# A two-layer encoder trunk on one Trainium2 core: queries placed by DMA, half of the FFN's sums moved into the projection ahead of it, and one pair of weights kept

## The chip, the cores and the metric

The kernel runs on one core of a Trainium2 chip. A core has TensorE for matrix products (PE in the profile, its weight loads PEld), VectorE (DVE), ScalarE (ACT), GpSimd (POOL) and SyncE (SP), which here only issues transfers. Each engine works through its own instructions in order and waits for the others by semaphores. The metric is the time of one execution on the device in microseconds (us); lower is better.

## The reference

One inference step for 1024 prompt tokens and 32 sample tokens of width 1024, two layers. Layer 0 mixes the tokens with a matrix-memory recurrence of 8 heads, layer 1 with windowed attention of 16 query heads over 2 key and value heads of 64. After each mixer comes a SwiGLU FFN (inner width 2816), and after each of the four sub-layers a normalisation:

```python
x = layer_norm(DEEPNORM_ALPHA * x + mix, ln_g[layer, 0], ln_b[layer, 0])
x = layer_norm(DEEPNORM_ALPHA * x + swiglu(x, w_gu[layer], w_down[layer]), ln_g[layer, 1], ln_b[layer, 1])

def swiglu(x, w_gu, w_down):
    g, u = jnp.split(x @ w_gu, 2, axis=-1)
    return (jax.nn.silu(g) * u) @ w_down
```

All is in float32, and the kernel returns the tokens after layer 1, the recurrence's states and the last keys and values.

## The kernel before

**Products.** A float32 operand is kept as two parts, a high one (a cast, on ACT) and a low one (the rest, a subtraction on DVE or POOL), and a product of two such operands is three matmuls, high by high, high by low, low by high (lines L360 to L362, `gemm`). The 1056 tokens lie along the columns, in transposed form: 8 tiles of 128 features (k) by 1056 columns. `ACT` (act) holds the values, `SX` (sx) their two parts.

**The order of the work.** The code is recorded as it is written, and `Weave` mixes it: a task is a generator that yields a pause in planned us of TensorE time, and every step of a `gemm` ticks that clock, so a task's instructions are put between matmuls. `drain` records a task's remaining part at once. Every engine then keeps this order. No wait or length seen on the chip changes it.

**Weights** (class `Weights`, L159 to L202). Units of 512 KB are loaded in a fixed order by SP into three raw buffers. Each unit is split into two halves, whose parts lie in one of five slots, or in a buffer of their own (`W.home`). A pair of units of the FFN makes seven factors for a fast 2 by 2 block product (seven products in place of eight). `done` frees a slot; while `W.ahead` is set, the next half is split some 1.7 planned us after the last one.

**The projection after a mixer** (`mixer_out`, L1135). The tokens go in four quarters of 264 columns; for each, 8 gemms of 24 matmuls, and then the quarter's normalisation as a task (`ln_task`, L421 to L474) that runs beside the next quarter's gemms: the mean by a matmul (L421), centring, squares, the variance by a matmul (L437), the scaling, and the split into sx (L468 on ACT, L474 on DVE and POOL). `squared` holds the quarters whose variance has been recorded. Of the fourth quarter's weights the first six units have their home in `E` (the tile ex).

**The FFN** (`ffn`). Of 22 inner tiles the first two are made plainly (`up_plain`, L1251 and L1253): a visit to tile i and token half c is four gemms of 24 matmuls, with the two units of that tile. The visits go (c 0, i 0), (c 0, i 1), (c 1, i 0), (c 1, i 1), and each visit loads and splits its two units, so each tile's units are loaded twice; these splits' low parts are DVE's (L202). From the third tile on, the block product is used (`up_tile`); its inputs are not only quarters of the tokens but sums of them: with x11, x21 the two feature halves of a half's first quarter and x12, x22 those of its second,

- t3 = x22 - x12, t2 = t3 + x11, t4 = x21 - t2, t1 = x12 - x11.

`sums` makes these for one half c, in steps of two tiles (128 x 528), as a task: a subtraction or addition on DVE into one of two buffers in z (L1287 to L1293), a cast on ACT (L1277), and the low part by turns on DVE and POOL (L1274). t2, t3 and t4 go to ex, t1 into sx in the place of x12, once the half's plain visits are done. Both tasks start after the fourth quarter's variance has been recorded, the second at the third visit, after `drain(tasks[3])`. The first fused tile uses them in the order t2, t4, t1, t3 (`summed`).

**Attention in layer 1.** The queries of a pair of heads j and a column block g (384, 384 and 288 columns) are a group; `q_group` projects it and writes Q so that a head's 64 features of high and of low parts stand in one 128-partition operand: ACT and DVE write 64 partitions each time, four operations (L1580 to L1585). The first four groups (block 0) are made while the last normalisation of layer 0 still runs; 20 more are made while the attention task works on the groups before, three units of 128 queries each (`scores` L1669 and L1675, `soft`, `turn` L1713 to L1717, `values`, `place` L1739). `q_made` tells the attention 2.0 planned us after a group that it may be used.

Of the kernel before, what the change touches and what calls it, by code (L numbers as in the profile page):

```python
# [16 lines left out]
P = 128  # L17
# [17 lines left out]
FIRST, TAIL = 2, 4  # L35
ALPHA = float((2 * DEPTH) ** 0.25)
# [204 lines left out]
def kernel(ctx: ExitStack, tc: tile.TileContext, A, O):  # L241
# [346 lines left out]
    def norm_tail(li, run, box, final=False):  # L588
# [3 lines left out]
        for g, (cols, (c, zs)) in enumerate(QUARTERS):  # L592
# [19 lines left out]
            tasks.append(wv.launch(ln_task(box[0].z, box[0].lnps, QUARTERS[g], li, last, final)))  # L612
        return tasks
# [437 lines left out]
    class Mixer(ExitStack):  # L1051
# [3 lines left out]
        def __init__(self, closing, us):  # L1055
# [8 lines left out]
            for i, u in enumerate(us):  # L1064
                for f in range(2):
                    W.home[u, f] = [self.E[:, h, 2 * i + f, : D // 2] for h in range(2)]

# [50 lines left out]
    def mixer_out(us, li, lx, opening=None, before=None):  # L1118
# [31 lines left out]
    def ffn(layer, li, tasks, lx, final):  # L1150
# [16 lines left out]
        def natural(k0, par):  # L1167
            return lambda c: SX[:, :, k0 : k0 + H, (2 * c + par) * N4 : (2 * c + par + 1) * N4]

        def extra(i):  # L1170
            return lambda c: E[:, :, H * i : H * (i + 1), c * N4 : (c + 1) * N4]

        X = {"x11": natural(0, 0), "x21": natural(H, 0), "x22": natural(H, 1), "t1": natural(0, 1)}
        extras = ("t2", "t3", "t4")
        X.update((o, extra(i)) for i, o in enumerate(extras))
# [62 lines left out]
        def up_plain(i, c):  # L1238
# [3 lines left out]
            for u in (ug, uu):  # L1242
                for par in range(2):
# [4 lines left out]
                    if par:  # L1248
                        W.done(u)
# [4 lines left out]

        plain = [False, False]
        made = []

        def sums(c):


            def x(k, par):
                return ACT[:, k : k + 2, group(2 * c + par)]

            todo = [(o, k) for k in range(0, H, 2) for o in ("t3", "t2", "t4")] + [("t1", k) for k in range(0, H, 2)]
            bufs = [Z[:, i : i + 2, c, :] for i in (7, 9)]
            while (li - 1, 3) not in squared:
                yield 0.3

            def halve(s, low):
                if 0 <= s < len(todo):  # L1270
                    o, k = todo[s]
                    d = X[o](c)[:, :, k : k + 2, :]
                    if low:
                        (nc.vector if s & 1 else nc.gpsimd).tensor_sub(d[:, 1], bufs[s % 2], d[:, 0].bitcast(F32))  # L1274
                        made.append((c, o))
                    else:
                        nc.scalar.copy(d[:, 0], bufs[s % 2])  # L1277

            for s in range(len(todo) + 2):
                halve(s - 2, True)  # L1280
                if s < len(todo):
                    o, k = todo[s]
                    while o == "t1" and not plain[c]:
                        yield 0.3
                    t, before = bufs[s % 2], bufs[(s - 1) % 2]
                    if o == "t3":
                        nc.vector.tensor_sub(t, x(k + H, 1), x(k, 1))  # L1287
                    elif o == "t2":
                        nc.vector.tensor_add(t, before, x(k, 0))
                    elif o == "t4":  # L1290
                        nc.vector.tensor_sub(t, x(k + H, 0), before)
                    else:
                        nc.vector.tensor_sub(t, x(k, 1), x(k, 0))  # L1293
                halve(s - 1, False)
                yield 2.6
# [64 lines left out]
        for c in range(2):  # L1360
            if c:
                wv.drain(tasks[3])
# [583 lines left out]
```

## Time and profile before

| | |
|---|---|
| median of three runs | 2261.14 us (2257.0 to 2265.25) |
| the profiled execution | 2258.92 us |
| its span | 2257.1 us |
| mean granted TensorE clock | 0.994 of full |
| PE busy | 2192.4 us, 97% |
| DVE, ACT, POOL busy | 66%, 45%, 48% |

The span runs from the first to the last instruction of the profiled execution; the time holds a little more around it. In rows of groups the number after x is the count, then come busy us, the mean of one in ns, and the idle time of the engine just before, with what ended it. Rows of waits give the total, the number and the longest. Rows in the order of time begin with start and length in us. Rows of a stretch give for each engine busy us and instructions, then the granted clock, the DMA engines' busy share and GB/s. An `L` with a number is a line of the kernel.

Layer 0's projection and normalisations lie at about 390 to 500 us, its FFN from there to 1175; the queries, keys and values and the attention at 1190 to 1455, layer 1's FFN start at about 1530.

### The profile page before, as it was taken

The numbers are of one execution on the slowest core, as the hardware profiler recorded it, in microseconds if no ns is written. First come the engines' busy times: TensorE is split into PE (matmuls) and PEld (weight loads), VectorE is DVE, ScalarE is ACT, GpSimd is POOL, SyncE is SP. The second block draws the span as 40 slices with busy tenths as digits, with TensorE's granted clock in tenths as the row PEclk, the third lists the DMA queues.
The fourth block names the chain that finished last, engine by engine and source line by source line (L and its number), as shares of the span: only waits on it lengthen the run. The fifth ranks groups of instructions, "written<-read, shape, count | busy, mean of one in ns | idle before, by whom it ended". The sixth has DMA issues, their size and how long they took to land.

```text
span 2257.1 us, 44139 instructions
## 1 busy us (share of the span) xinstructions
PE 2192.4 (97%) x17086; PEld 2152.2 (95%) x17086; DVE 1490.2 (66%) x2850; ACT 1016.2 (45%) x2285; POOL 1076.8 (48%) x999
## 2 busy tenths in 40 slices
PE   9999999999999999999998999899999999999997
PEld 9899999998999999999997998899999999999997
DVE  4465577778566665566667789887666665466657
ACT  4443345464444444322246788656444444422124
POOL 2544331016666666544326775412666666654422
PEclk9999999999999999999999999999999999999999
DMA  4222112211434443696424211421344344397712
GB/s 148 76 51 69 53 39 94 87 48 67 163 135 143 152 149 138 233 329 230 154 77 139 79 60 44 136 74 47 115 153 149 133 148 154 126 343 249 256 50 77
DMA packets 167394, 291.52 MB, mean 129 GB/s; under 512 B 16593, under 2 KB 123145, under 8 KB 167185
## 3 DMA queue, kind: packets, MB, share of 16 engines
q1 hardware_dynamic: 162832, 284.38, 37.1%
q10 hardware_dynamic: 4352, 4.33, 0.5%
q8 instruction: 134, 2.20, 0.4%
q14 instruction: 76, 0.61, 0.1%
HBM read 203.89 MB, written 82.94 MB: 127 GB/s over the span
## 4 chain that ended last, share of the span: by engine, by line
PE 80%; DVE 8%; ACT 4%; DMA 3%; issue 3%; POOL 1%; SPq 0%; ACTq 0%; DVEq 0%; POOLq 0%
PE A L360 9%; PE A L362 9%; PE A L361 9%; PE d L360 9%; PE d L362 9%; PE d L361 9%; PE B L360 7%; PE B L361 7%; PE B L362 7%; PE T L1713 1%; DMA sx<-hs_t 1%; DVE wl L202 1%; DMA wr<-in_dn 1%; DVE ex L1274 1%; PE T L904 1%
## 5 line engine op out<-in xcount | busy, mean ns | idle before, releaser
L202 POOL TENSOR_TENSOR wl_s<-wr,wh_s 128x512 fp32r<-128x512 f32 x224 | 316.6, 1434 | 241.0 <-ACT wh_s L200 169.0
L360 PE MATMUL d<-sx,wh 128*128 128x264 f32 (+2 forms) x1068 | 341.1, 319 | 2.2 <-DVE z L1253 1.5
L362 PE MATMUL d<-sx,wl 128*128 128x264 f32 (+2 forms) x1068 | 326.5, 306 | 7.7 <-DVE wl L202 5.5
L361 PE MATMUL d<-sx,wh 128*128 128x264 f32 (+2 forms) x1068 | 325.7, 305 | 2.0 <-DVE sx L474 1.1
L200 ACT CAST wh_s<-wr 128x512 fp32r<-128x512 f32 x224 | 135.4, 617 | 317.0 <-DVE wr L177 289.1
L360 PE MATMUL A<-sx,wh_s 128*128 128x264 f32 x896 | 255.2, 285 | 2.8 <-ACT z L1338 2.8
L361 PE MATMUL A<-sx,wh_s 128*128 128x264 f32 x896 | 254.8, 284 | 0.0
L362 PE MATMUL A<-sx,wl_s 128*128 128x264 f32 x896 | 254.7, 284 | 0.0
L362 PEld LDWEIGHTS d<-sx,wl 128*128 128x128 f32 x1068 | 201.7, 189 | 10.1 <-DVE wl L202 7.1
L360 PEld LDWEIGHTS d<-sx,wh 128*128 128x128 f32 x1068 | 202.4, 189 | 6.0 <-issue 2.2
L361 PEld LDWEIGHTS d<-sx,wh 128*128 128x128 f32 x1068 | 202.5, 190 | 4.3 <-POOL sx L474 1.5
L202 POOL TENSOR_TENSOR wl_a<-wr,wh_a 128x512 fp32r<-128x512 f32 x112 | 169.1, 1516 | 51.4 <-ACT wh_a L200 49.8
L202 POOL TENSOR_TENSOR wl<-wr,wh 128x512 fp32r<-128x512 f32 (+2 forms) x75 | 100.1, 1343 | 173.9 <-ACT wh L200 151.3
L360 PE MATMUL d<-sx,ex 128*128 128x264 f32 x624 | 180.7, 290 | 0.4 <-ACT sx L390 0.2
L362 PE MATMUL d<-sx,ex 128*128 128x264 f32 x624 | 177.9, 285 | 3.1 <-DVE ex L202 2.6
L361 PE MATMUL d<-sx,ex 128*128 128x264 f32 x624 | 177.3, 284 | 0.2 <-DVE sx L391 0.2
L360 PEld LDWEIGHTS A<-sx,wh_s 128*128 128x128 f32 x896 | 169.0, 189 | 3.3 <-ACT z L1338 3.3
L362 PEld LDWEIGHTS A<-sx,wl_s 128*128 128x128 f32 x896 | 169.4, 189 | 0.0
L361 PEld LDWEIGHTS A<-sx,wh_s 128*128 128x128 f32 x896 | 169.0, 189 | 0.0
L1693 POOL TENSOR_SCALAR s<-s,st 128x256 f32<-128x256 f32 (+1 forms) x144 | 125.5, 884 | 67.4 <-DVE st L1691 54.7
L1208 POOL TENSOR_TENSOR z<-z 128x528 fp32r<-128x528 f32 x76 | 105.2, 1384 | 107.2 <-issue 55.5
L1207 ACT CAST z<-z 128x528 fp32r<-128x528 f32 x136 | 85.9, 631 | 95.9 <-DVE z L1220 46.0
(334 smaller groups left out, 7389.7 us busy)
## 6 DMA issues: line engine op xcount, KB each, us to landing
wr<-in_gu SPq DMA_DIRECT2D x96, 512.0 KB, 4.6
hs_x<-z SPq DMA_DIRECT2D x72, 528.0 KB, 2.8
hs_t<-z SPq DMA_DIRECT2D x64, 528.0 KB, 4.0
sx<-hs_x SPq DMA_DIRECT2D x112, 264.0 KB, 6.0
sx<-hs_t SPq DMA_DIRECT2D x64, 264.0 KB, 5.9
ex<-hs_t SPq DMA_DIRECT2D x64, 264.0 KB, 6.1
wr<-in_dn SPq DMA_DIRECT2D x32, 512.0 KB, 5.5
ex<-hs_x SPq DMA_DIRECT2D x32, 264.0 KB, 6.1
```

What stands on the lines that cost most here:

```text
L200: self.nc.scalar.copy(hi, r)
L202: eng.tensor_sub(lo, r, hi.bitcast(F32))
L360: nc.tensor.matmul(out, ah, bh, start=start and k == 0, stop=False, **kw)
L361: nc.tensor.matmul(out, ah, bl, start=False, stop=False, **kw)
L362: nc.tensor.matmul(out, al, bh, start=False, stop=stop and k == last, **kw)
L904: nc.tensor.matmul(pc[:, : 2 * (DV + 1)], keys, vt[j][:L, c], start=True, stop=True)
L1207: nc.scalar.copy(hi.bitcast(F32R), buf(s))
L1208: eng.tensor_sub(lo.bitcast(F32R), buf(s), hi)
L1274: (nc.vector if s & 1 else nc.gpsimd).tensor_sub(d[:, 1], bufs[s % 2], d[:, 0].bitcast(F32))
L1693: nc.gpsimd.tensor_scalar_mul(p[:R, h, lo:256], p[:R, h, lo:256], st[:R, 2, h : h + 1])
L1713: nc.tensor.transpose(pt[:nk, i, h, :R], p[:R, h, c : c + nk], ident[:R, :R])
```

## The change

Five places change.

- **Visits.** They go (0, 0), (0, 1), (1, 1), (1, 0). The second plain tile's two units are loaded and split once and held over two visits (four of five slots); the first tile's are loaded twice as before.
- **Sums of the first half.** `sums` moves out of `ffn`. For half 0 it is started at the head of the fourth quarter's projection, after the second quarter's normalisation has been recorded to its end, with two buffers of its own (su) in a small pool. The six units in E lie in another order, so that the places of t2 and t4 come free first; `lx.left` counts the units that have been used, and a step waits, when recorded, until its place is free. From the seventh step on it waits for the fourth quarter's variance.
- **Order of the sums.** t3's base is made without a split first (`raw`), for t2 and t4; t3 itself is made again and split after them, then t1. So each half has ten steps on DVE and not eight, and as many casts and low parts as before. The pauses are 2.4 planned us for half 0 and 2.2 for half 1, from 2.6.
- **Half 1** starts, as before, at the third visit after `drain(tasks[3])`, with its buffers in z.
- **Queries.** ACT makes the high part (qh) and DVE the low part (ql) of all 128 partitions in one operation each; a task then issues four transfers from SP, each of 64 partitions, into Q. `q_made` waits 4.0 planned us. Before the attention begins, the last of the first four groups' transfers has been recorded.

```diff
+VISITS = [(0, i) for i in range(FIRST)] + [(1, i) for i in reversed(range(FIRST))]
@@ add_ffn
-        for c in range(2):
-            for i in range(FIRST):
-                up[i, c] = [add("gu", 2 * (layer * FT + i) + k) for k in range(2)]
+        for c, i in VISITS:
+            held = up.get((i, 1 - c)) if i == FIRST - 1 else None
+            up[i, c] = held or [add("gu", 2 * (layer * FT + i) + k) for k in range(2)]
@@ Mixer
-            for i, u in enumerate(us):
+            self.made, self.plain, self.left = [], [False, False], 0
+            for i, u in zip((0, 4, 1, 5, 2, 3), us):
@@ sums (moved out of ffn)
-            todo = [(o, k) for k in range(0, H, 2) for o in ("t3", "t2", "t4")] + [("t1", k) for k in range(0, H, 2)]
-            while (li - 1, 3) not in squared:
-                yield 0.3
+        todo = [(o, k) for k in range(0, H, 2) for o in ("raw", "t2", "t4")]
+        todo += [(o, k) for o in ("t3", "t1") for k in range(0, H, 2)]
+        for s in range(len(todo) + 2):
+            if not c and s >= 6:
+                while (li, 3) not in squared:
+                    yield 0.3
+            halve(s - 2, True)
+            if s < len(todo):
+                o, k = todo[s]
+                while o == "t1" and not lx.plain[c]:
+                    yield 0.3
+                while not c and lx.left < {"t2": 1, "t4": 2}.get(o, 0) + k:
+                    yield 0.3
...
+            halve(s - 1, False)
+            yield pause
@@ mixer_out, run
+            if g == 3:
+                lx = box[0]
+                lx.sums = ExitStack()
+                su = lx.sums.enter_context(pool("sums"))
+                bufs = [new(su, f"su{i}", [P, 2, N4])[:] for i in range(2)]
+                wv.drain(lx.norms[1])
+                lx.comb = wv.launch(sums(lx, li, 0, bufs, 2.4))
...
+                if g == 3 and (u, 0) in W.home:
+                    box[0].left += 1
@@ up_plain
-                    if par:
+                    if par and (c or i < FIRST - 1):
                         W.done(u)
@@ ffn
-            combs.append(wv.launch(sums(c)))
-            for i in range(FIRST):
-                up_plain(i, c)
-            plain[c] = True
+        combs = [lx.comb]
+        for c, i in VISITS:
+            if (c, i) == (1, FIRST - 1):
+                wv.drain(tasks[3])
+                combs.append(wv.launch(sums(lx, li - 1, 1, [Z[:, i : i + 2, 1, :] for i in (7, 9)], 2.2)))
+            up_plain(i, c)
+            lx.plain[c] = (c, i) in (VISITS[FIRST - 1], VISITS[-1])
@@ q_group
-        nc.scalar.activation(q[0:64, 0, :n], ps[0:64], AF.Copy, scale=sc)
-        nc.scalar.activation(q[64:128, 1, :n], ps[64:128], AF.Copy, scale=sc)
...
+        nc.scalar.activation(h, ps, AF.Copy, scale=sc)
+        nc.vector.scalar_tensor_tensor(l, ps, sc, h.bitcast(F32), op0=ALU.mult, op1=ALU.subtract)
+
+        def place():
+            yield 1.0
+            for i in range(2):
+                own, other = slice(64 * i, 64 * i + 64), slice(64 - 64 * i, 128 - 64 * i)
+                nc.sync.dma_start(q[own, i, :n].bitcast(F32), h[own].bitcast(F32))
+                nc.sync.dma_start(q[other, i, :n].bitcast(F32), l[own].bitcast(F32))
+
+        return wv.launch(place())
@@ main
+    wv.drain(placing)
...
     def q_made():
-        yield 2.0
+        yield 4.0
```

Lines from about 290 on have other numbers in the changed kernel: L202 is L203 there, L426 L427, L1135 L1202, L1253 L1315, L1274 L1100, L1277 L1103, L1287 L1118, L1289 L1120, L1291 L1122, L1293 L1124.

DVE in the fourth quarter's projection of layer 0, before (L1135 adds a gemm's result to act; L430, L433 and L600 are a normalisation's):

```order
L1135 SCALAR_TENSOR_TENSOR act<-act,d_5737 128x264
L426 TENSOR_TENSOR act<-ln_5717,act 128x2x264
L430 TENSOR_TENSOR z_4627<-z_4627 128x2x264
L202 TENSOR_TENSOR wl_0_5787<-wr_5062,wh_0_5786 128x512
L430 TENSOR_TENSOR z_4627<-z_4627 128x2x264
L1135 SCALAR_TENSOR_TENSOR act<-act,d_5773 128x264
L600 TENSOR_TENSOR z_4627<-act 128x2x264
L433 TENSOR_TENSOR z_4627<-z_4627 128x264
L1135 SCALAR_TENSOR_TENSOR act<-act,d_5810 128x264
```

The same place in the changed kernel:

```order
L1202 SCALAR_TENSOR_TENSOR act<-act,d_5743 128x264
L427 TENSOR_TENSOR act<-ln_5723,act 128x2x264
L431 TENSOR_TENSOR z_4627<-z_4627 128x2x264
L1120 TENSOR_TENSOR su_675_5673<-su_674_5672,act 128x528
L203 TENSOR_TENSOR wl_0_5794<-wr_5062,wh_0_5793 128x512
L431 TENSOR_TENSOR z_4627<-z_4627 128x2x264
L1202 SCALAR_TENSOR_TENSOR act<-act,d_5779 128x264
L601 TENSOR_TENSOR z_4627<-act 128x2x264
L1122 TENSOR_TENSOR su_674_5672<-act,su_675_5673 128x528
L434 TENSOR_TENSOR z_4627<-z_4627 128x264
L1100 TENSOR_TENSOR ex_4623<-su_675_5673,ex_4623 128x2x264
L1118 TENSOR_TENSOR su_675_5673<-act 128x528
```

Sums of the first half (su) and a low part (L1100 into ex) now stand among the normalisation's work; from the quarter's first gemm to its last they are seven rows.

DVE at the third visit of the plain tiles in layer 0, before:

```order
L474 TENSOR_TENSOR sx<-act,sx 128x2x264
L1274 TENSOR_TENSOR ex_4623<-z_4627,ex_4623 128x2x264
L1287 TENSOR_TENSOR z_4627<-act 128x2x264
L1253 TENSOR_TENSOR z_4627<-z_4627,d_6199 128x264
L202 TENSOR_TENSOR wl_1_6240<-wr_6011,wh_1_6239 128x512
L1287 TENSOR_TENSOR z_4627<-act 128x2x264
L202 TENSOR_TENSOR wl_0_6265<-wr_6082,wh_0_6264 128x512
L1289 TENSOR_TENSOR z_4627<-z_4627,act 128x2x264 x2
L1274 TENSOR_TENSOR ex_4623<-z_4627,ex_4623 128x2x264
L1291 TENSOR_TENSOR z_4627<-act,z_4627 128x2x264 x2
L202 TENSOR_TENSOR wl_1_6314<-wr_6082,wh_1_6313 128x512
```

And in the changed kernel:

```order
L475 TENSOR_TENSOR sx<-act,sx 128x2x264
L1315 TENSOR_TENSOR z_4627<-z_4627,d_6206 128x264
L1124 TENSOR_TENSOR su_674_5672<-act 128x528
L1118 TENSOR_TENSOR z_4627<-act 128x2x264
L1120 TENSOR_TENSOR z_4627<-z_4627,act 128x2x264
L1100 TENSOR_TENSOR ex_4623<-su_675_5673,ex_4623 128x2x264
L1124 TENSOR_TENSOR su_675_5673<-act 128x528
L1122 TENSOR_TENSOR z_4627<-act,z_4627 128x2x264
L203 TENSOR_TENSOR wl_1_6307<-wr_5765,wh_1_6306 128x512
L1100 TENSOR_TENSOR ex_4623<-z_4627,ex_4623 128x2x264
```

Fewer low halves of weights (wl) stand here, and the first half has only t3 and t1 left. From the fourth norm's scaling (L447) to the first fused tile's first addition (L1326) 48 instructions stood on DVE, now 41 do: 3 low halves of weights and not 7, 13 sums and not 15, 6 low parts of sums and not 7, the rest alike.

SP where the first group of the second column block is made, before:

```order
L1774 DMA out_p_v<-act 128x128
L1775 DMA out_s_v<-act 128x32
L159 DMA wr_14805<-in_wqb 128x1024
L1607 DMA bt_14893<-in_bias 128x2x256
L1608 DMA sb_14894<-in_bias 32x2x160
L159 DMA wr_14936<-in_wqb 128x1024
```

And in the changed kernel:

```order
L1799 DMA out_p_v<-act 128x128
L1800 DMA out_s_v<-act 128x32
L160 DMA wr_14811<-in_wqb 128x1024
L1608 DMA Q_14868<-qh_14869 64x384
L1609 DMA Q_14868<-ql_14870 64x384
L1608 DMA Q_14868<-qh_14869 64x384
L1609 DMA Q_14868<-ql_14870 64x384
L160 DMA wr_14919<-in_wqb 128x1024
```

The group's four transfers stand between two weight loads; the bias loads come after the second group's transfers.

More of the change, by code (lines that the diff above doesn't have):

```diff
@@ L1165, in bank @@
             return new(px.pool[tag], tag, [P, 2, 512], bufs=2)[:, :, :N4]
[L1167 to L1173, printed above, removed]
+        X = seven(E)
         extras = ("t2", "t3", "t4")
-        X.update((o, extra(i)) for i, o in enumerate(extras))
         def tiles(t):
@@ L1253, in up_plain @@
                         nc.vector.tensor_mul(t, t, ps)
[L1255 to L1262, printed above, removed]
-            todo = [(o, k) for k in range(0, H, 2) for o in ("t3", "t2", "t4")] + [("t1", k) for k in range(0, H, 2)]
-            bufs = [Z[:, i : i + 2, c, :] for i in (7, 9)]
-            while (li - 1, 3) not in squared:
-                yield 0.3
[L1269 to L1295, printed above, removed]
         tail = []
@@ L1373, in summed @@
             for c in range(2):
-                wv.drain(combs[c], lambda: o != "t1" and made.count((c, o)) == 2)
+                wv.drain(combs[c], lambda: o != "t1" and lx.made.count((c, o)) == 2)
             if o == "t1":
+                lx.sums.close()
                 staging.append(wv.launch(stage(0)))
@@ L1578, in q_group @@
         q = Q[j, g] = new(pb, "Q", [P, 2, 384], F32R, bufs=4)
+        h, l = (new(pb, tag, [P, 384], F32R, bufs=2)[:, :n] for tag in ("qh", "ql"))
         sc = -(HD ** -0.5)
[L1580 to L1587 removed]
+        nc.scalar.activation(h, ps, AF.Copy, scale=sc)
[7 more added lines that the diff above has]
+        return wv.launch(place())
     ck = new(pb, "ck", [P, P])
@@ L1627 @@
     for j in range(4):
-        q_group(j, 0)
+        placing = q_group(j, 0)
         W.done(U_QB[0][j])
```

41 lines of the change are left out of this document (32 added, 9 removed).

## The prediction

> **What bounds the kernel now.** I read the page first, then the chain of waits, then the busy time of the engines in stretches of the span, and last the waits of TensorE and the order of time in the stretches that lose.
>
> ```profile
> PE 2192.4 (97%) x17086; PEld 2152.2 (95%) x17086; DVE 1490.2 (66%) x2850; ACT 1016.2 (45%) x2285; POOL 1076.8 (48%) x999
> PE 80%; DVE 8%; ACT 4%; DMA 3%; issue 3%; POOL 1%; SPq 0%; ACTq 0%; DVEq 0%; POOLq 0%
> ```
>
> TensorE is the bound, and no matmul is removed. What can be won is only time in which TensorE stands still, and 8% of the chain is on VectorE (DVE). Where that is shows in the stretches (length, then busy time and instructions of PE, PEld, DVE, ACT, POOL, then the granted clock):
>
> ```profile
> 462.00:487.00 25.00, 25.00 (x206) 24.86 (x205) 18.88 (x32) 14.17 (x25) 5.24 (x4) 1.00 0.13 44
> 510.00:550.00 40.00, 34.55 (x265) 32.49 (x264) 35.99 (x39) 19.94 (x38) 25.36 (x16) 1.00 0.16 53
> 1560.00:1600.00 40.00, 34.51 (x265) 32.45 (x264) 36.37 (x40) 20.33 (x39) 25.36 (x16) 1.00 0.17 54
> 501.00:545.40 44.40, 38.95 (x301) 36.89 (x300) 42.35 (x48) 25.36 (x48) 22.97 (x14) 1.00 0.14 48
> ```
>
> In 462 to 487, the fourth quarter's projection, TensorE issues 206 matmuls in 25 us, 8.24 in a us. In 510 to 550, where layer 0's FFN starts, it issues 265 where 40 x 8.24 = 330 would fit: 65 too few, or 7.8 us. Layer 1's start (1560 to 1600) loses the same 7.8 us. In 501 to 545.4, from the fourth norm's scaling to the first fused tile's first addition, DVE is busy 42.35 of 44.4 us with 48 operations, 0.88 us each, at full clock. TensorE's own waits there:
>
> ```profile
> PE d L362 <- DVE wl L202: 2.8, 3, 1.2
> PE A L360 <- ACT z L1321: 0.8, 1, 0.8
> PE d L360 <- DVE z L1253: 0.7, 1, 0.7
> PE d L361 <- DVE sx L474: 0.5, 1, 0.5
> ```
>
> Three of the four are for DVE, among them the low halves of the plain pairs' weights (wl), which stand in DVE's queue behind the sums. The fourth, ScalarE's copy L1321, stands behind casts that wait for DVE.
>
> **The change, part by part: the start of the FFN.** What DVE does there, by groups:
>
> ```profile
> L1274 DVE TENSOR_TENSOR ex<-z,ex 128x528 fp32r<-128x528 f32 x6 | 8.7, 1446 | 0.0
> L202 DVE TENSOR_TENSOR wl<-wr,wh 128x512 fp32r<-128x512 f32 x7 | 4.8, 682 | 1.6 <-ACT wh L200 1.6
> L1287 DVE TENSOR_TENSOR z<-act 128x528 f32<-128x528 f32 x3 | 4.1, 1375 | 0.1
> L1293 DVE TENSOR_TENSOR z<-act 128x528 f32<-128x528 f32 x4 | 3.8, 942 | 0.1
> L447 DVE SCALAR_TENSOR_TENSOR z<-ln,eps_ln,z 128x264 f32<-128x264 f32 x1 | 0.5, 492 | 3.5 <-ACT z L445 3.5
> ```
>
> By the order of the changed kernel 41 operations stand on DVE between the same two points, not 48. Four weight splits fall away (the second pair's weights are kept: 4 x 0.68 = 2.7 us), one low half has gone ahead (1.4), and of 15 subtractions 13 are left (2 of about 1.1: 2.2), though the second half now makes two more, since t3's base is made twice. That is 6.4 us; by the mean, 7 x 0.88 = 6.2. DVE then has 41 x 0.88 = 36.2 us to do where TensorE's 301 matmuls need 301 / 8.24 = 36.5 us. The two come out level, so the queue no longer falls behind as a whole, but single waits stay (the norm's own chain, the first tile's ScalarE copy). The gain lies between 2.7 us (the weights alone) and all 7.8; I take 5.5, nearer to the 6.2 of work than to the loss, less one wait of 0.7. Two layers: 11 us. The two weight loads of 512 KB and four ScalarE casts a layer that fall away with them cost nothing before either: the DMA share is 0.16, and ACT is busy 19.94 of 40 us. The weights kept hold four of the five slots in two visits; the last visit's weights are then split during the third, two gemms before their use. I cost that at nothing; the third visit's 96 matmuls (96 / 8.24 = 11.7 us) cover them.
>
> **The fourth quarter's projection** takes what is moved: seven DVE operations per layer, of 0.7 us when nothing else runs (4.9), three casts on ACT (25.00 - 14.17 leaves it 10.8 us) and one low half on POOL. DVE has 25.00 - 18.88 = 6.1 us idle there, so they fit if they fall into the gaps. What is late next, should they not, is the fourth norm's mean:
>
> ```profile
> 484.33 1.44 DVE L602 TENSOR_TENSOR z<-z 128x264 f32<-128x264 f32 x1
> 486.98 0.60 PE L421 MATMUL ln<-z,onesm 128*128 128x264 f32 x2
> ```
>
> DVE finishes its sum at 485.77, TensorE needs it at 486.98: 1.2 us of slack. DVE operations do not always last 0.7:
>
> ```profile
> 511.92 1.64 POOL L474 TENSOR_TENSOR sx<-act,sx 128x528 fp32r<-128x528 f32 x1 [1.06 <-ACT sx L468]
> 511.68 0.70 DVE L474 TENSOR_TENSOR sx<-act,sx 128x528 fp32r<-128x528 f32 x1
> 512.30 1.82 DVE L1274 TENSOR_TENSOR ex<-z,ex 128x528 fp32r<-128x528 f32 x1
> ```
>
> One that was under way when POOL began took 0.70, the next, begun while POOL ran, 1.82. POOL is busy only 5.24 of these 25 us, so one or two of the seven meet it: 4.9 + 2 x 1.1 = 7.1 us against 6.1 idle and 1.2 of slack. The bounds are 0 and, if all seven lasted 1.82 (12.7 - 6.1 - 1.2), 5.4 us a layer; I take 0.5, so 1 us for both. The Trainium skill (SBUF — State Buffer, section "SBUF: two separate sides") speaks against this part: VectorE operations with two SBUF inputs and GpSimd share a port pair under an exclusive lock, and the loser blocks for the whole instruction. The two rows above agree. By that rule each of the seven could cost a whole POOL operation, and the sum would be that of the first rival below.
>
> **The queries.** For each of 24 groups two ScalarE and two DVE operations on 64 partitions become one each on 128, then four transfers.
>
> ```profile
> L1580 ACT ACTIVATE Q<-d x24: 384/481/486, 1208.2 to 1409.3; 64x384 fp32r<-64x384 f32 x16, 64x288 fp32r<-64x288 f32 x8
> L1585 DVE SCALAR_TENSOR_TENSOR Q<-d,Q x24: 459/559/561, 1211.8 to 1410.8; 64x384 fp32r<-64x384 f32 x16, 64x288 fp32r<-64x288 f32 x8
> L1540 DVE TENSOR_TENSOR KL<-d,KH 128x384 fp32r<-128x384 f32 x2 | 1.1, 552 | 1.8 <-ACT KH L1539 1.8
> PE T L1713 <- DVE lo L1717: 3.9, 2, 2.3
> PE T L1713 <- DVE st L1691: 1.3, 3, 0.7
> PE psS L1669 <- DVE st L1675: 5.6, 1, 5.6
> ```
>
> The time does not hang on the partitions: the keys' split on 128 x 384 takes 552 ns, the queries' on 64 x 384 takes 559. So 0.48 us goes from ACT and 0.56 from DVE per group. In the attention (1260 to 1420, the first two rows of waits) TensorE waits 5.2 us for DVE in five pieces. If each piece gets shorter by the half us that one query group saves on DVE, 2.5 us: I take that, between 0 and 5.2. At the attention's start TensorE waits 5.6 us once, for the first reduction, which stands on DVE behind the last norm and four query groups:
>
> ```profile
> 1214.35 0.55 DVE L1582 SCALAR_TENSOR_TENSOR Q<-d,Q 64x384 fp32r<-64x384 f32 x1 [2.01 <-ACT Q L1581]
> 1215.50 0.49 DVE L447 SCALAR_TENSOR_TENSOR z<-ln,eps_ln,z 128x264 f32<-128x264 f32 x1
> 1226.39 0.55 DVE L1582 SCALAR_TENSOR_TENSOR Q<-d,Q 64x384 fp32r<-64x384 f32 x1 [0.55 <-ACT Q L1581]
> ```
>
> The second group's pair delays the norm (L447): without its second ACT and DVE operation L447 starts 1.0 us sooner. The third saves 0.56, the last about 0.6. I take 2.0 of these 2.2 (bounds 0 and 5.6).
>
> The transfers are added to SP's queue, and the first scores wait for them. The worst place is the first group of the second column block:
>
> ```profile
> 1266.14 0.56 DVE L1585 SCALAR_TENSOR_TENSOR Q<-d,Q 64x384 fp32r<-64x384 f32 x1
> 1267.23 0.28 PE L1669 MATMUL psS<-KH,Q 128*128 128x256 f32 x1
> 1265.81 0.38 SPq L159 DMA_DIRECT2D wr<-in_wqb  x1
> 1203.21 0.60 SPq L1548 DMA_DIRECT2D KL<-KL  x1
> KH<-KH SPq DMA_DIRECT2D x6, 96.0 KB, 4.1
> KL<-KL SPq DMA_DIRECT2D x6, 96.0 KB, 2.2
> ```
>
> Today the scores follow the split by 0.5 us. In the changed kernel their place is 2 us later (4.0 for 2.0), 1269.2. The transfers can be issued from 1266.2, behind a weight load, at about 0.55 us each until 1268.4; the key halves of the same size landed 2.2 to 4.1 us after issue. The group is complete between 1270.6 and 1272.5, and TensorE waits 1.4 to 3.3; the rows with a weight load just ahead are the slower ones, but the first head needs only the first two: I take 2.0. What queues behind on SP are weight and bias loads; a group adds 2.2 us of issue in some 8 us, and weights are loaded three units ahead, so I cost the rest at nothing. By the Trainium skill (DMA: Bandwidth & Descriptors, section "Anatomy of one DMA") a transfer takes some 2.0 us plus its bytes at 436 GB/s, an estimate of 2.2 us for 96 KB: KL agrees, KH does not, and the wait would be 1.4.
>
> **The sum.** -11.0 + 1.0 - 2.5 - 2.0 + 2.0 = -12.5 us. The profiled execution took 2258.9 us (span 2257.1), so 2246.4; the median of the three runs is 2261.1, 0.1% above it, so 2248.6 is predicted.
>
> **The rivals.**
> First: the moved sums make DVE late in the fourth quarter. If most of the seven meet POOL, the fourth norm's mean is 5.4 us late, the third visit waits for its output (L474), and the start's gain is eaten: -12.5 + 2 x (5.4 - 0.5) = -2.7, so 2258. The 1.82 us row speaks for it, POOL's 5.24 busy us against it.
> Second: the start waits less for DVE's load than for single chains, and only the kept weights' splits help: -2 x 2.7 + 1.0 - 2.5 = -7, so 2254. For it: three waits are for wl alone.
> Third, slower: SP. Its queue is in order, so a query's transfers stand behind a weight load that waits for its buffer, and later loads behind transfers that wait for DVE's split. If that makes each of the 20 later groups, or the weights behind them, 1.2 us late for TensorE, +24 us stand against 15.5 won (11.0 + 2.5 + 2.0): 2261.1 - 15.5 + 24 = 2270. It decides from 15.5 / 20, about 0.8 us a group. For it: SP issues transfers without a pause from 1255 to 1267, each 0.5 us. Against it: only the first group today follows its split so closely, and attention runs about two groups behind the projections.
>
> **How the numbers follow.** Forecast 0.60, first rival 0.12, second 0.12, third 0.16. 0.3% of 2261 is 6.8 us, about what a measurement here tells from no change. Faster by more: the forecast and a third of the second rival, 0.64. Within: the first and the rest of the second, 0.19. Slower: 0.17. The range: below, everything at its good bound (-15.6 - 2.5 - 2.2, no costs) gives 2241; above, 2264 takes in both middle rivals and leaves out most of the third. The forecast's own range is 2241 to 2254.
>
> **What would show it.** Between 510 and 550 (and its twin 1050 us later) some 45 more matmuls, no wait for wl in the third visit, DVE no longer at 9.9 of 10 us. In the fourth quarter DVE busy 24 of 25 us, and TensorE's mean L421 (now L422) without a wait: a wait of over 2 us there is the first rival. At the attention's start a first reduction 2 us sooner, and one wait of some 2 us for a query transfer; such waits at many groups, or waits for weights, are the third. The forecast is wrong if TensorE's loss at the two starts stays above 5 us.

## The result: 7.8 us faster, where 12.5 were forecast

| | before | after |
|---|---|---|
| median of 11 runs each | 2261.43 us (2257.0 to 2265.39) | 2253.62 us (2249.85 to 2255.64) |
| ratio | | 0.9964, 95% interval 0.9954 to 0.9974 |
| span of the profiled execution | 2257.1 us | 2252.2 us |

Predicted were 2248.6 us, between 2241 and 2264. The sign and the range held; of 12.5 us forecast, 7.8 came. The 23 us of that range hold both middle rivals too, so to lie inside it says little.

The page of the kernel after, engines and chain:

```profile
PE 2190.7 (97%) x17086; PEld 2152.6 (96%) x17086; DVE 1465.9 (65%) x2826; ACT 999.1 (44%) x2253; POOL 1069.6 (47%) x999
PE 77%; DVE 9%; ACT 5%; DMA 4%; issue 2%; POOL 2%; SPq 0%; DVEq 0%; POOLq 0%; ACTq 0%
```

VectorE does 24 us less than before, and still its share of the chain has not fallen (9%, before 8%). ScalarE's and GpSimd's have grown by a point each. The stretches of the kernel after (columns as in the prediction; the windows of the two starts are taken 5 and 10 us earlier than there; in layer 0 the fourth norm's scaling now stands at 504.05, before at 500.96, and the first fused tile's first addition at 542.29, before at 544.67):

```profile
462.00:487.00 25.00, 24.79 (x201) 24.44 (x201) 24.15 (x37) 13.91 (x26) 5.21 (x4) 1.00 0.15 44
505.00:545.00 40.00, 37.11 (x293) 36.35 (x292) 30.37 (x41) 21.61 (x41) 17.46 (x13) 0.98 0.10 28
1550.00:1590.00 40.00, 37.05 (x291) 36.30 (x291) 30.55 (x41) 21.81 (x41) 17.47 (x13) 0.97 0.08 27
504.00:542.30 38.30, 35.42 (x286) 34.70 (x284) 29.18 (x41) 20.53 (x40) 15.14 (x11) 1.00 0.10 28
```

At the two starts 293 and 291 matmuls stand where 330 would fit at 8.24 a us: 4.5 and 4.7 us lost in place of 7.8. By these windows the gain is 3.3 and 3.1 us, not 5.5 each, and 28 and 26 more matmuls, not some 45. The last row runs from the fourth norm's scaling to the first fused tile's first addition, as the prediction's 501 to 545.4 did: 41 operations on DVE, as foreseen, but only 29.18 busy us in 38.3. VectorE now stands idle there for 9.1 us and is late all the same.

The two windows of the starts end inside a stretch in which TensorE's granted clock is half (0.98 and 0.97 on average; the last section). So the same matmuls are compared as well, 503 of them, from just ahead of the fourth norm's scaling to behind that stretch: the kernel before, the kernel after, and start_alone, an experiment below with the same start, whose trace has no such stretch there.

```profile
499.40:568.30 68.90, 63.45 (x503) 61.39 (x502) 54.71 (x63) 37.54 (x71) 39.45 (x26) 1.00 0.20 69
502.00:568.30 66.30, 63.41 (x503) 62.65 (x502) 42.18 (x56) 33.56 (x63) 32.77 (x24) 0.97 0.17 57
501.30:566.10 64.80, 61.94 (x503) 61.18 (x502) 42.19 (x56) 33.61 (x63) 32.73 (x24) 1.00 0.18 58
```

The start gains 2.6 us with the stretch and 4.1 without it. In layer 1 it is 2.6 and 4.0 (69.0, 66.4 and 65.0 us).

TensorE's waits in the kernel after, at the first start (480 to 560), around the attention's start (1195 to 1240) and in the attention (1245 to 1455):

```profile
PE A L361 <- ACT z L1341: 2.6, 1, 2.6
PE ln L422 <- DVE z L603: 0.3, 1, 0.3
PE d L362 <- POOL sx L475: 0.2, 1, 0.2
...
PE psS L1693 <- DVE st L1699: 3.9, 2, 3.1
...
PE T L1737 <- DVE st L1715: 5.3, 5, 1.7
PE T L1737 <- DVE lo L1741: 4.8, 5, 2.2
...
PE psS L1693 <- DMA Q<-qh: 0.5, 1, 0.5
PE psS L1693 <- DMA Q<-ql: 0.2, 1, 0.2
```

The waits for wl are gone. In their place is one wait of 2.6 us at the first fused tile, for ScalarE's copy L1341 (L1321 before, where it was 0.8). Layer 1 shows the same wait, 2.7 us. What leads to it is in the chain of waits between 525 and 546 (start, length, what):

```profile
528.03 1.45 POOL wl_a L203
529.49 1.29 POOL ex L1100
530.78 2.25 issue
533.07 0.49 POOL wl_a L203
533.56 1.03 issue
534.59 1.35 POOL ex L1100
535.97 1.78 DVE z L1124
537.75 0.63 DVE ex L1100
538.40 0.71 DVE z L1124
539.11 0.61 DVE wr L177
539.82 0.70 DVE wr L178
540.74 0.40 issue
541.15 0.61 ACT wh_s L201
```

and in the order of time on GpSimd and VectorE there, with the idle time before each and what ended it:

```profile
528.03 1.45 POOL L203 TENSOR_TENSOR wl_a<-wr,wh_a 128x512 fp32r<-128x512 f32 x1 [4.75 <-PE d L363]
529.45 1.33 POOL L1100 TENSOR_TENSOR ex<-z,ex 128x528 fp32r<-128x528 f32 x1
...
530.81 0.71 DVE L1118 TENSOR_TENSOR z<-act 128x528 f32<-128x528 f32 x1 [2.48 <-POOL ex L1100]
535.97 1.78 DVE L1124 TENSOR_TENSOR z<-act 128x528 f32<-128x528 f32 x1 [1.59 <-POOL ex L1100]
```

L1118 to L1124 are the sums' subtractions, L1100 their low parts, L203 the weights' low parts. A sum's low part on GpSimd (L1100) stands behind the first fused pair's split, ahead of which GpSimd was idle for 4.75 us, by the view until TensorE was done with a weight slot. ScalarE's cast of the same weights, which the split also needs, had ended only just before, at 527.95:

```profile
527.34 0.61 ACT L201 CAST wh_a<-wr 128x512 fp32r<-128x512 f32 x1
```

So without the slot the split could have begun 0.1 us sooner at most. VectorE's next subtraction waits for the buffer which that low part reads, twice, 4.1 us together. Behind it in VectorE's queue stand t1's sums (L1124) and L177 and L178, which make the weights of the third of the seven products; ScalarE's casts wait for L178 and the copy L1341 stands behind them. That was the first theory: GpSimd, held up by the slot, hands buffers back late, and VectorE's order passes that on to the weights.

### The profile page after: what moved, and what is told of

Same layout as the page of the kernel before. It is cut to its first block, busy times and chain, and to the rows that moved or that the text cites. A ratio compares the mean times of both kernels' runs of the same rounds, so it can differ in the third digit from the quotient of the medians.

```text
span 2252.2 us, 44278 instructions
## 1 busy us (share of the span) xinstructions
PE 2190.7 (97%) x17086; PEld 2152.6 (96%) x17086; DVE 1465.9 (65%) x2826; ACT 999.1 (44%) x2253; POOL 1069.6 (47%) x999
## 4 chain that ended last, share of the span: by engine, by line
PE 77%; DVE 9%; ACT 5%; DMA 4%; issue 2%; POOL 2%; SPq 0%; DVEq 0%; POOLq 0%; ACTq 0%
PE A L361 9%; PE A L363 9%; PE A L362 9%; PE d L361 8%; PE d L363 8%; PE d L362 8%; PE B L361 7%; PE B L362 7%; PE B L363 7%; DMA wr<-in_dn 1%; PE T L1737 1%; DMA sx<-hs_t 1%; ACT act L463 1%; DVE wl L203 1%; POOL wl L203 1%
## 5 line engine op out<-in xcount | busy, mean ns | idle before, releaser
L203 POOL TENSOR_TENSOR wl_s<-wr,wh_s 128x512 fp32r<-128x512 f32 x224 | 314.9, 1426 | 242.6 <-ACT wh_s L201 183.2
L203 POOL TENSOR_TENSOR wl_a<-wr,wh_a 128x512 fp32r<-128x512 f32 x112 | 169.2, 1518 | 58.7 <-ACT wh_a L201 47.7
L203 POOL TENSOR_TENSOR wl<-wr,wh 128x512 fp32r<-128x512 f32 (+2 forms) x75 | 100.1, 1344 | 179.2 <-ACT wh L201 156.1
L361 PE MATMUL A<-ex,wh_s 128*128 128x264 f32 x448 | 129.1, 288 | 5.3 <-ACT z L1341 5.3
```

The costliest lines, as they stand in the source:

```text
L203: eng.tensor_sub(lo, r, hi.bitcast(F32))
L361: nc.tensor.matmul(out, ah, bh, start=start and k == 0, stop=False, **kw)
```

## The experiments

All changes are against the kernel after where nothing else is said. Ratios are to the kernel before, which stood at 2261.45, 2262.96 and 2261.65 us beside the three groups of runs. Differences between two ratios are turned into us with 2261.4. Some of the expectations speak of a wait of 2.8 us at the first fused tile and a stretch of 1.7 us at half clock; the views have 2.6 and 2.7 us, and some 3.4 us at half clock, which cost 1.4 (the last section).

| run | median us | ratio, 95% interval |
|---|---|---|
| start_alone | 2255.32 | 0.9972 (0.9961 to 0.9983) |
| queries_alone | 2259.90 | 0.9988 (0.9979 to 0.9996) |
| pair_not_kept | 2259.28 | 0.9987 (0.9977 to 0.9996) |
| pair_kept_alone | 2257.98 | 0.9981 (0.9972 to 0.9989) |
| split_later | 2255.54 | 0.9961 (0.9949 to 0.9973) |
| low_on_vector | 2248.30 | 0.9934 (0.9920 to 0.9947) |
| t1_later | 2250.31 | 0.9946 (0.9931 to 0.9960) |
| t1_split_later | 2249.95 | 0.9940 (0.9928 to 0.9952) |
| low_on_gpsimd | 2258.08 | 0.9982 (0.9971 to 0.9994) |
| low_t1_later | 2245.72 | 0.9925 (0.9911 to 0.9939) |
| low_not_kept | 2253.47 | 0.9958 (0.9944 to 0.9973) |
| low_shared_t3 | 2248.35 | 0.9938 (0.9924 to 0.9953) |

### The parts apart

**The start without the queries** (start_alone):

```diff
-        h, l = (new(pb, tag, [P, 384], F32R, bufs=2)[:, :n] for tag in ("qh", "ql"))
...
+        nc.scalar.activation(q[0:64, 0, :n], ps[0:64], AF.Copy, scale=sc)
...
     def q_made():
-        yield 4.0
+        yield 2.0
```

> The changed kernel with the queries made and placed by the engines as before, so the sums and the kept pair alone. The prediction gave the two starts -11.0 + 1.0 = -10.0 us against before. The trace of the changed kernel shows the start losing 4.5 us in place of 7.8 us in each layer, so the reading now (a new 2.8 us wait and a 1.7 us stretch at half clock in each) expects about 2 x -3.3 = -6.6 us, less what the fourth quarter's projection costs, so -5 to -6 us: some 2256 us. If it is -9 or more, the start did all that was forecast and the queries cost time.

6.1 us faster than the kernel before, by the medians, and not the 10 that the prediction gave it.

**The queries alone**, the same lines put into the kernel before (queries_alone).

> The kernel before with nothing but the queries placed by transfers. The prediction gave it -2.0 (first reduction) -2.5 (attention) +2.0 (wait for a transfer) = -2.5 us. By the waits of the changed kernel's trace it is -2.5 -1.0 +0.7 = -2.8 us. The rival that the transfers queue up and make each group late says +9 us.

1.6 us faster by the medians, 0.9 to 4.7 by the ratio's interval. The two parts add up: 6.1 + 1.6 = 7.7. TensorE waits for transfers once for qh, 1.8 us, and once for ql, 0.2 us, and for no others between 1200 and 1440.

**The pair not kept**:

```diff
-            held = up.get((i, 1 - c)) if i == FIRST - 1 else None
+            held = None
...
-                    if par and (c or i < FIRST - 1):
+                    if par:
```

> The changed kernel, except that the second plain pair's weights are loaded and split anew for its second visit: four subtractions of 0.69 us come back to VectorE in each layer. If VectorE's load sets the end of the start (the prediction's reading), each layer loses those 2.8 us: +5.5 us against the changed kernel. If VectorE waits there for GpSimd anyway (4.1 us idle in the last 13 us of the stretch), most of them fit into that idle time: at most +2 us.

The ratio rises from 0.9964 to 0.9987: 5.2 us, close to the 5.5 of the first reading. So the four subtractions count in full, although VectorE has idle time. They stand in its queue ahead of L178, and the idle time, which ends when GpSimd is done with a buffer, comes at other places. TensorE's waits at the first start in this kernel:

```profile
PE A L361 <- ACT z L1341: 3.7, 1, 3.7
PE d L362 <- DVE sx L475: 1.0, 1, 1.0
```

What is left here, the queries and the moved sums, comes to 0.9987, the queries alone to 0.9988. In this state of things the moved sums win nothing that can be measured.

**The kept pair alone**, in the kernel before:

```diff
...
+            held = up.get((i, 1 - c)) if i == FIRST - 1 else None
+            up[i, c] = held or [add("gu", 2 * (layer * FT + i) + k) for k in range(2)]
...
```

> The kernel before with the kept pair alone, its sums where they were. VectorE's load as the limit: four subtractions of 0.69 us fewer in each layer, and the waits for the split weights of the third visit (2.8 us in the trace of before) gone: -5.5 us. If what VectorE no longer does only uncovers a wait for something else: -1 to -3 us.

3.5 us by the medians, 4.3 by the ratio: between the two expectations. The waits for wl shrink from 2.8 to 1.7 us, and the one for ScalarE's copy stays at 0.8.

### What holds the start

**The split later on GpSimd** (split_later), so that it stands behind two of the sums' low parts:

```diff
...
-        key = self.jobs[self.njob]
-        u, f = key
+        key = u, f = self.jobs[self.njob]
+        if key == self.hold: return False
...
-            ug, uu = up[i, c]
+            ug, uu = up[i, c]; W.hold = (up[FIRST], "a1")
...
+                        W.hold = None if (c, i, par) == (1, 0, 1) else W.hold; nc.scalar.activation(t, ps, AF.Silu)
```

> The changed kernel, with the first fused factor's split issued behind two of the sums' low parts on GpSimd, in place of ahead of them, where it stands 4.8 us for a weight slot that TensorE still reads. If this wait makes the start late, VectorE's waits for GpSimd (2.5 and 1.6 us) go, its subtractions for the first fused pair end up to 4 us sooner, and the wait of 2.8 us at the first fused tile with the half-clock stretch behind it (1.7 us) goes in both layers: -6 to -9 us against the changed kernel. If what counts is that VectorE has the t1 sums ahead of those subtractions, or the order on ScalarE, -0 to -2 us.

Nothing: 0.9961 against 0.9964. The split no longer stands ahead of the sums, and TensorE's wait is still 2.7 us. VectorE in this kernel:

```profile
526.96 1.85 DVE L1122 TENSOR_TENSOR z<-act,z 128x528 f32<-128x528 f32 x1
532.50 1.80 DVE L174 TENSOR_TENSOR wr<-wr,wr 128x512 f32<-128x512 f32 x1 [1.18 <-POOL wl_a L203]
535.94 1.79 DVE L1100 TENSOR_TENSOR ex<-z,ex 128x528 fp32r<-128x528 f32 x1
539.17 0.69 DVE L178 TENSOR_TENSOR wr<-wr,wr 128x512 f32<-128x512 f32 x1
```

It now waits at L174, which overwrites the raw weights that GpSimd's later split still reads, and three of its operations last 1.8 us in place of 0.7, each begun while GpSimd ran. L178 comes at 539.17 against 539.82, but all of this kernel's rows stand 0.7 us earlier already at 511. The slot was the visible end of the chain and not what it hangs on; that part of the theory fell.

**The second half's low parts on VectorE** (low_on_vector), four more of 0.7 us in each layer:

```diff
-                    (nc.vector if s & 1 else nc.gpsimd).tensor_sub(d[:, 1], bufs[s % 2], d[:, 0].bitcast(F32))
+                    (nc.vector if c or s & 1 else nc.gpsimd).tensor_sub(d[:, 1], bufs[s % 2], d[:, 0].bitcast(F32))
```

> The changed kernel with all low parts of the second half's sums on VectorE: four more subtractions of 0.7 us there in each layer, and no sum behind the weight slot on GpSimd. If the wait for the slot decides, VectorE gains 4.1 us of idle time and pays 2.8: the wait at the first fused tile shrinks by 1.3 us, -3 to -6 us for both layers with a part of the half-clock stretches. If VectorE's load decides: +5.6 us.

6.8 us faster than the kernel after (0.9934 against 0.9964, the intervals do not meet): more work on the engine which the prediction took for the limit, and less time, even less than was expected. The two starts, and TensorE's longest wait at the first:

```profile
505.00:545.00 40.00, 38.81 (x311) 37.88 (x310) 31.41 (x44) 21.76 (x42) 15.98 (x12) 1.00 0.14 40
1550.00:1590.00 40.00, 38.82 (x312) 37.88 (x311) 30.06 (x42) 20.07 (x39) 16.53 (x12) 1.00 0.18 54
PE A L361 <- ACT z L1341: 0.7, 1, 0.7
```

2.3 and 2.2 us are lost where it was 4.5 and 4.7. VectorE's mean operation lasts 31.41 / 44 = 0.71 us in the first, against 30.37 / 41 = 0.74. On GpSimd no sum stands behind the split here, and the idle time ahead of the split now ends with ScalarE's cast, not with the slot:

```profile
526.64 1.45 POOL L203 TENSOR_TENSOR wl_a<-wr,wh_a 128x512 fp32r<-128x512 f32 x1 [9.11 <-ACT wh_a L201]
```

At full clock over the whole start, some 500 matmuls like those above take 63.2 us, 66.3 in the kernel after and 64.8 in start_alone: of the 3.1 us that a start wins, about half is the half-clock stretch that does not come.

**t1's sums later** (t1_later): they may be recorded only when the third product is reached, behind L177 and L178.

```diff
-            lx.plain[c] = (c, i) in (VISITS[FIRST - 1], VISITS[-1])
+            lx.plain[c] = (c, i) == VISITS[FIRST - 1] or lx.plain[c]
...
         def summed(o):
+            lx.plain[1] = True
```

> The changed kernel with the second half's t1 sums behind the first fused pair's own subtractions on VectorE (t1 is read only by the fifth of the seven products): 3.2 us of work and a wait of 1.6 us for GpSimd no longer stand ahead of the subtraction that the third product's weights come from. If that chain on VectorE decides, the wait of 2.8 us and the half-clock stretch go in both layers: -7 to -9 us against the changed kernel. If the wait for the slot on GpSimd decides it through another path, at most -3 us.

4.1 us faster than the kernel after (0.9946 against 0.9964, the intervals overlap a little). TensorE's wait at the copy falls to 0.4 and 0.5 us, one of 0.4 comes at a later copy (L1358). At the first start:

```profile
PE A L361 <- ACT z L1341: 0.4, 1, 0.4
```

Less than expected, but it goes with the chain: VectorE's order ahead of L178 sets the end.

**Both** (t1_later and split_later, t1_split_later).

> Both edits together. If each alone does away with the same wait, no more than the better of the two; if each takes a part, their sum, with the start's loss of 4.5 us in each layer as the limit: at most -9 us against the changed kernel, 2245 us.

0.9940, within the interval of t1_later: the split's place adds nothing here either.

### How much is GpSimd, how much VectorE's work

**All low parts of the second half on GpSimd** (low_on_gpsimd):

```diff
+                    (nc.vector if s & 1 and not c else nc.gpsimd).tensor_sub(d[:, 1], bufs[s % 2], d[:, 0].bitcast(F32))
```

> The changed kernel with all low parts of the second half's sums on GpSimd: four subtractions of 0.7 us fewer on VectorE in each layer, and four more sums whose buffer comes back only from GpSimd's queue. If VectorE's work sets the start, -3 to -5.6 us against the changed kernel. If what VectorE waits for on GpSimd sets it (the run with all of them on VectorE says so), each more makes it later: the wait at the first fused tile grows from 2.8 us to 4 us or more in both layers, +2 to +8 us.

4.1 us slower than the kernel after (0.9982 against 0.9964, the intervals overlap a little), with less work on VectorE. TensorE's wait there, and VectorE's waits:

```profile
PE A L361 <- ACT z L1341: 4.2, 1, 4.2
...
530.08 2.43 DVE L1118 TENSOR_TENSOR z<-act 128x528 f32<-128x528 f32 x2 [2.49 <-POOL ex L1100]
536.05 1.78 DVE L1124 TENSOR_TENSOR z<-act 128x528 f32<-128x528 f32 x1 [2.26 <-POOL ex L1100]
539.04 0.71 DVE L1124 TENSOR_TENSOR z<-act 128x528 f32<-128x528 f32 x1 [1.21 <-POOL ex L1100]
```

Three waits for GpSimd where there were two. With the low parts by turns, all on VectorE and all on GpSimd the wait at the copy is 2.6, 0.7 and 4.2 us: where the sums' low parts are made sets the wait. That it is the handing over of the buffers, and not that the same step takes 1.3 us and more on GpSimd and 0.7 on VectorE, or that VectorE's operations last 1.8 us beside GpSimd, is argued from the order of the rows; a third buffer, which would take the hand-over away alone, was not tried.

**Low parts on VectorE, the pair not kept** (low_not_kept: the edits of both).

> The changed kernel with the low parts on VectorE and the second plain pair's weights split anew: VectorE has four more subtractions of 0.69 us in each layer and no idle time left to put them into. If VectorE's load is what the kept pair relieves: +5.5 us against the run with the low parts on VectorE and the pair kept. If the kept pair only counted because of the waits for GpSimd: +0 to +2 us.

5.4 us slower than with the pair kept (0.9958 against 0.9934, again with a little overlap). Without the waits for GpSimd the four subtractions cost as much as with them. And the moved sums, which won nothing in pair_not_kept, now come with a gain: this kernel has them, the queries and the low parts on VectorE and not the pair, 0.9958, where the queries alone have 0.9988: 6.8 us, and the intervals do not meet. What the low parts on VectorE would give without the moved sums was not run.

**Low parts on VectorE and t1 later** (low_t1_later: the edits of both).

> The changed kernel with the low parts on VectorE and with the t1 sums behind the first fused pair's subtractions. What is left of the wait at the first fused tile with the low parts on VectorE alone is 0.7 us in each layer, so at most -1.5 us against that run: 2246 to 2249 us. If VectorE, with 2.8 us more work, is now late for the fifth product's sums, up to +3 us.

2245.72 us, 0.9925 (0.9911 to 0.9939): the lowest median of all, 15.9 us below the kernel before, and faster than the kernel after beyond both intervals. Against low_on_vector the 2 us are within the uncertainty, but its trace shows the wait gone. The two starts and all that TensorE waits for at the first:

```profile
505.00:545.00 40.00, 39.75 (x324) 39.24 (x323) 32.96 (x44) 21.52 (x42) 15.76 (x11) 1.00 0.15 44
1550.00:1590.00 40.00, 39.71 (x323) 39.20 (x323) 32.94 (x45) 20.45 (x40) 15.81 (x11) 1.00 0.18 54
PE ln L422 <- DVE z L603: 0.3, 1, 0.3
PE d L362 <- POOL sx L475: 0.2, 1, 0.2
```

0.7 and 0.8 us lost in 40: of the 7.8 us of before, 7 are won in each layer.

**Low parts on VectorE, the second half's sums in the old order** (low_shared_t3: t3 first, its difference used again, two subtractions fewer).

```diff
+        todo = [(o, k) for k in range(0, H, 2) for o in ("t3", "t2", "t4")] + [("t1", k) for k in range(0, H, 2)] if c else todo + [(o, k) for o in ("t3", "t1") for k in range(0, H, 2)]
```

> The changed kernel with the low parts on VectorE, and with the second half's sums in their old order, in which t3 stands first and its difference is used again: two subtractions of 0.7 us fewer in each layer. By VectorE's load at most the 0.7 us that is left of the wait: -1.4 us against the run with the low parts on VectorE; if t2 and t4 now come late because t3 is split ahead of them, up to +3 us.

0.9938 against 0.9934, no difference in time. In the trace the wait of 0.7 us at the copy is gone, which the new order can have done as well as the two subtractions; the 1.4 us for both layers are less than the interval. A sixth weight slot was not tried.

## Why the prediction was right and where it was wrong

**The start of the FFN: forecast -5.5 a layer, found -3.3 and -3.1 by the windows.** Over the same matmuls it is -2.6, or -4.1 and -4.0 where no half-clock stretch follows. This is the step that failed. The count was right (41 operations), and so was "single waits stay (the norm's own chain, the first tile's ScalarE copy)". Wrong was what such a wait would come to. The sum put down 41 operations at a mean of 0.88 us against TensorE's 36.5 us and took the 6.2 us of work that leaves VectorE as the gain, "less one wait of 0.7". In the trace the 41 take 29.18 us, 0.71 each, so the load would have let nearly all 7.8 us go; but the wait that stays is 2.6 us, because VectorE idles 4.1 us for buffers that GpSimd holds and L178 stands behind. Before, VectorE had no idle time there in which such waits could show (42.35 of 44.4 us busy). With the low parts and t1 moved, 7 us of 7.8 are won. The forecast's own sign of being wrong, a loss above 5 us at the starts, was missed narrowly: 4.5 and 4.7 us by the windows, and 5.3 at the first (66.30 - 503 / 8.24) with the whole half-clock stretch.

**The second rival** had "single chains" and "only the kept weights' splits help", 2254 us, at a chance of 0.12. The time was 2253.6, and the kept pair gave 5.2 of the 7.8 us (its price in the rival was 5.4; alone, in the kernel before, it gave 3.5 to 4.3). It named the mechanism better than the forecast did. What it did not have is the condition: with the second half's low parts on VectorE, and so GpSimd out of the way, these and the moved sums are worth 6.8 us together.

**The held slots at nothing** is not contradicted: TensorE has no wait for a split of the last visit, and taking the sums out from behind the split that stood 4.75 us won nothing (split_later).

**The fourth quarter: forecast +0.5 a layer.** DVE is busy 24.15 of 25 us, as foreseen, and TensorE issues 201 matmuls where it was 206, 0.6 us. Just ahead of the 503 matmuls compared above, some 300 take 38.2 us where they took 37.2 (463.8 to 502.0, before 462.2 to 499.4), and in layer 1 37.9 where they took 37.0 (1506.0 to 1543.9, before 1509.5 to 1546.5): +1.0 and some +0.9. The fourth norm's mean waits 0.3 us. The first rival (5.4 us) did not come. The rule that VectorE's two-input operations and GpSimd lock each other out (the Trainium skill, SBUF — State Buffer, section "SBUF: two separate sides") shows in single rows, 0.71 us without and 1.8 with GpSimd at work, but POOL's 5.21 busy us there left it little room. It bit at the start of the FFN instead, where GpSimd is busy 17.46 of 40 us: L1124 took 1.78 us.

**The queries: forecast -2.5, found -1.6**, with the terms shifted. The first reduction's wait fell from 5.6 to 3.1 us, 2.5 where 2.0 were forecast. The attention's waits for DVE did not get shorter: for the two kinds of piece that the prediction counted, TensorE waited 9.8 us in ten pieces between 1250 and 1460 before,

```profile
PE T L1713 <- DVE lo L1717: 7.1, 5, 2.3
PE T L1713 <- DVE st L1691: 2.7, 5, 0.8
```

and 10.1 after (1245 to 1455). Those for lo shrank by 2.3 us, those for st grew by 2.6, though VectorE is busy 164.55 of these 210 us where it was 174.54, ScalarE 158.55 where it was 166.95. In the narrower window that the prediction took they were 5.2 us and are 4.7 (1255 to 1415). "Each piece gets shorter by the half us" was wrong: these waits did not go with the engine's load. What sets them was not tried. The wait for a transfer was 0.7 us, not 2.0. The transfers were issued from 1264.13, and the scores of the first head began at 1268.56, 4.4 us later, those of the second at 1269.21, 5.1 later: inside the forecast's 4.4 to 6.3 for the whole group. TensorE reached that place 4.0 us after the first issue, not 3.0. The section of the Trainium skill from which the prediction worked out 2.2 us for a transfer gives its fit for transfers that GpSimd issues; these are SyncE's, and the medians from issue to landing here are 4.0 us for qh and 2.2 for ql, at 96 KB each. The third rival, SP, did not come.

**The sum.** By the windows the terms come to -6.4 + 1.2 - 2.5 + 0.3 + 0.7 = -6.7 us, against 7.8 measured. That they come so near is in part luck, as the spans of the two traces differ by 4.9 us only. Over the same matmuls start_alone's trace gives -4.1 - 4.0 + 1.0 + 0.9 = -6.2 us for the two starts and fourth quarters; by the medians that run is 6.1 us faster. The range's lower end, 2241, is not "everything at its good bound": with the prediction's own bounds of 5.2 and 5.6 us in place of 2.5 and 2.2 it would be 2235.

## What to carry to other kernels

A queue that is 95% busy is not shown to be short of capacity: ask, for each operation that stands ahead of the late one, which engine must give its buffer back, and price those hand-overs apart from the work. Spreading small steps over two engines by turns can cost more than doing them all on the busier one, if two buffers alternate between them. And order counts like load: what the next engine waits for should not stand behind work that is needed two products later.

## What the hardware showed that was not expected

TensorE's clock falls to half for some 3 us soon after short waits, but not each time. After the waits of 2.6 and 2.7 us at the first fused tile the kernel after shows, at the two starts,

```profile
543.30:546.70 3.40, 3.40 (x18) 3.40 (x17) 1.10 (x1) 1.06 (x3) 3.40 (x3) 0.50 0.49 153
1588.10:1591.20 3.10, 3.10 (x15) 3.10 (x16) 1.50 (x2) 1.46 (x3) 3.10 (x3) 0.50 0.28 100
```

a granted clock of 0.50, 18 matmuls in 3.4 us. With the same waits, start_alone kept the full clock at both places; the first:

```profile
542.70:546.10 3.40, 3.40 (x30) 3.40 (x29) 1.03 (x1) 2.10 (x4) 3.40 (x3) 1.00 0.51 154
```

The stretch so costs (30 - 18) / 8.8 = 1.4 us where it comes (8.8 a us is the rate of the row with 30). The profiled execution of the kernel before has one at 579.4 to 582.9 (granted 0.52), behind 9.4 us in which TensorE is busy 7.60. The Trainium skill (TensorE: Matmul & The Clock Gate, section "Part 1: The HAM clock gate") puts the fall after an idle window of some 3.4 us that runs freely. The length of the stretch agrees, and a window that runs freely would fit that the same wait has it or not; the waits here are shorter than that window. Which of them are followed by it was not settled. One execution can therefore lie some us off its kernel's median: of low_on_vector's, the two with a mean granted clock of 0.997 took 2244.10 and 2245.55 us, the two with 0.994 2252.02 and 2253.98, and start_alone's profiled execution, with 0.992, took 2261.23 where the median is 2255.32. A difference of two single traces is not that of the kernels: between before and after it is 4.9 us in the spans and 7.8 in the medians.
